# Row sums of 16,384 rows on one core: 16-row blocks, loads alternating between two rings, a last block in shrinking pieces

## The chip, the cores and the metric

One core of one Trainium2 chip runs the kernel. The metric is the device time of one execution in microseconds (us); the span of a run in its profile is 1.6 to 2.1 us shorter. All runs quoted are fast (the granted clock is 1.0 in all), and most runs of one kernel lie within 0.3% of one another. Ratios and their intervals compare fast runs of the same rounds on the same chip, and differ by less than 0.001 from the ratio of the medians quoted beside them.

Names: VectorE is DVE in the profile and ScalarE is ACT. SyncE (SP) only issues loads and stores here. "SPq" and "ACTq" are the instruction sequencers of SyncE and ScalarE, which issue transfers; each feeds a ring (a queue of transfers) of its own, and both rings are served by the same 16 DMA engines. A load "lands" when it is reported complete, some 0.4 us after its last packet ends.

## The reference, cut to what matters

```python
batch, seq, dim = 32, 512, 1024           # x: float32, 67.1 MB
def reference(x, multiplier):             # multiplier = 0.5
    return (np.sum(x, axis=-1) * multiplier).astype(np.float32)
```

Each of the 128 partitions owns 128 consecutive rows of 4 KiB, so any group of n rows is one contiguous run of n x 4 KiB per partition.

## The kernel before

It loads 15 blocks of 8 rows per partition (4 MiB each) through three buffers, all from SyncE's ring, and then a taper of 2, 2, 1, 1, 1, 1 rows. VectorE reduces seven rows of each block in one instruction, and ScalarE sums the eighth with an activation that accumulates.

```python
taper = [(2, "s"), (2, "s"), (1, "s"), (1, "v"), (1, "v"), (1, "v")]
big_rows = 8
big_pool = ctx.enter_context(tc.tile_pool(name="big", bufs=3))
...
for _ in range(n_big):                                    # 15 times
    x_tile = big_pool.tile([P, big_rows, D], fp32, name="x_tile_b")
    nc.sync.dma_start(out=x_tile, in_=x_rows[:, c0 : c0 + big_rows, :])
    nc.vector.reduce_sum(out=staging[:, c0 : c0 + 7], in_=x_tile[:, 0:7, :], ...)
    nc.vector.tensor_single_scalar(...)                   # times 0.5
    scalar_row_sum(x_tile, 7, c0 + 7)                     # ScalarE: one row
    c0 += big_rows
for sz, eng in taper:
    ...                                                   # load sz rows, sum on ScalarE or VectorE
nc.sync.dma_start(out=out_view, in_=out_sbuf)
```

The compiled program is not laid out in source order: the framework orders each engine's instructions itself. Each engine works its list off in order: in e11 below VectorE leaves a block that landed at 134.78 us untouched until 142.07, since an earlier block in its list had not landed.

## Time and profile before

The median of the first three runs was 164.76 us.

| | before |
|---|---|
| span of the profiled run | 163.1 us |
| a 32 KiB packet (one partition's 8 rows), median of the packet records | 1,213 ns |
| packet time per DMA engine, sum of the records over 16 | 157.6 us |
| big blocks land every | 9.7 to 9.85 us |
| reduction of 7 rows on VectorE | 7.62 us |
| last landing of data, then to the end | 159.82 us, 3.3 us |

From the page of the kernel before: the span, the busy time of the engines, then two rows with one value for each of 40 equal slices of the span (the busy tenths of the DMA engines, and the GB/s they moved), the share of the ring, and the costliest group.

```profile
span 163.1 us, 170 instructions
...
DVE 118.8 (73%) x36; ACT 23.9 (15%) x41; POOL 0.2 (0%) x4
...
DMA  6999999999999999999999999999999999998990
GB/s 193 442 402 458 434 386 466 426 394 466 418 402 466 426 394 466 434 410 466 410 450 434 402 466 426 410 458 426 426 450 410 434 450 402 466 426 368 413 382 19
...
q1 hardware_dynamic: 3168, 67.18, 96.6%
...
L78 DVE TENSOR_REDUCE staging<-x_tile_b 128x7 f32<-128x7168 f32 x15 | 114.3, 7620 | 40.3 <-DMA x_tile_b<-in_x_dram 40.3
```

The DMA row is the one to read: 9 tenths or more from the second slice to nearly the last. A packet of 32 KiB in 1,213 ns on each of 16 engines is 432 GB/s. The Trainium skill ("DMA: Bandwidth & Descriptors", "Where 436 GB/s comes from") puts the ceiling of the ports into SBUF at 435 GB/s, and the trace agrees; the lower figure that the same section gives for loads from HBM, about 358 GB/s, does not limit this run on one core. VectorE's last column says what it waits for: 40.3 us in all, always the load.

The chain of waits of the kernel before (start, length, what), that is, the chain of work that ended last:

```profile
by line: DMA x_tile_b<-in_x_dram 58.8%; DVE staging L78 18.7%; DMA x_tile_s<-in_x_dram 17.6%; SPq L97 1.3%; SPq L76 0.7%; DVE x_tile_s L62 0.4%; issue 0.4%; DVEq L137 0.0%
...
33.02 7.63 DVE staging L78
40.66 0.02 SPq L76
...
40.71 21.65 DMA x_tile_b<-in_x_dram
...
62.38 7.63 DVE staging L78
...
131.09 28.73 DMA x_tile_s<-in_x_dram
...
159.85 0.69 DVE x_tile_s L62
```

The chain alternates between 21 us of transfer and 7.63 us of reduction, which looks as if VectorE were on the path for 19% of the span. It is not: the reduction frees a buffer and so starts a load, but two other loads are queued in that time, and the engines stay full. The chain shows who released whom; whether a resource ran dry is seen only in the row of slices.

Its last line is the sum of the last row on VectorE, 0.69 us, right after the last landing.

### The profile page before, as it was taken

The page shows a single profiled execution, that of the slowest core. Times are in us where ns is not written, and L with a number is a line of the kernel's source. Part 1 is how long each engine was busy: PE and PEld are TensorE (multiplying, and loading weights), DVE is VectorE, ACT ScalarE, POOL GpSimd, SP SyncE. Part 2 cuts the span into 40 slices and gives each one's busy share as a digit, 9 for nine tenths or more (in the row PEclk, how much of TensorE's full clock was granted, in tenths as well). Part 3 has the DMA queues.
Part 4 walks back from the last instruction along what each step waited for, and adds up shares of the span by engine and source line. Part 5 has one row for each costly group of instructions (what it writes and reads, how often), then busy time and mean ns, then how long its engine had stood idle before and what let it go on. Part 6 is the DMA issues. An engine that isn't in the chain of part 4 may idle for free.

```text
span 163.1 us, 170 instructions
## 1 busy us (share of the span) xinstructions
DVE 118.8 (73%) x36; ACT 23.9 (15%) x41; POOL 0.2 (0%) x4
## 2 busy tenths in 40 slices
DVE  0007949699595987959599595977959598695982
ACT  3002020020200202020020201102020020202670
POOL 0000000000000000000000000000000000000000
DMA  6999999999999999999999999999999999998990
GB/s 193 442 402 458 434 386 466 426 394 466 418 402 466 426 394 466 434 410 466 410 450 434 402 466 426 410 458 426 426 450 410 434 450 402 466 426 368 413 382 19
DMA packets 3168, 67.18 MB, mean 412 GB/s; under 512 B 352, under 2 KB 480, under 8 KB 992
## 3 DMA queue, kind: packets, MB, share of 16 engines
q1 hardware_dynamic: 3168, 67.18, 96.6%
HBM read 67.11 MB, written 0.07 MB: 412 GB/s over the span
## 4 chain that ended last, share of the span: by engine, by line
DMA 76%; DVE 19%; SPq 2%; issue 0%; DVEq 0%
DMA x_tile_b<-in_x_dram 59%; DVE staging L78 19%; DMA x_tile_s<-in_x_dram 18%; SPq L97 1%; SPq L76 1%; DVE x_tile_s L62 0%; DVEq L137 0%
## 5 line engine op out<-in xcount | busy, mean ns | idle before, releaser
L78 DVE TENSOR_REDUCE staging<-x_tile_b 128x7 f32<-128x7168 f32 x15 | 114.3, 7620 | 40.3 <-DMA x_tile_b<-in_x_dram 40.3
L53 ACT ACTIVATE x_tile_b<-x_tile_b 128x1024 f32<-128x1024 f32 x15 | 15.8, 1057 | 131.8 <-DMA x_tile_b<-in_x_dram 131.8
L53 ACT ACTIVATE x_tile_s<-x_tile_s 128x1024 f32<-128x1024 f32 x5 | 5.2, 1046 | 1.6 <-DMA x_tile_s<-in_x_dram 1.6
L83 DVE TENSOR_SCALAR out_sbuf<-staging 128x7 f32<-128x7 f32 x15 | 2.6, 170 | 0.5
L53 ACT ACTIVATION_READ_ACCUMULATOR x_tile_b<-x_tile_b 128x1 f32 x15 | 2.8, 187 | 0.0
L62 DVE CUSTOM_DVE_ANT_0 x_tile_s<-x_tile_s 128x512 f32<-128x512 f32 x3 | 2.1, 689 | 0.9 <-DMA x_tile_s<-in_x_dram 0.9
L53 ACT ACT_TABLE_LOAD x1 | 1.3, 1283 | 0.7 <-PEq L123 0.7
L53 ACT ACTIVATION_READ_ACCUMULATOR x_tile_s<-x_tile_s 128x1 f32 x5 | 0.9, 186 | 0.0
L62 DVE DVE_READ_ACCUMULATOR2_ANT out_sbuf<- 128x1 f32 x3 | 0.2, 82 | 0.0
L123 POOL MEMSET const-uint8-127<- 128x1 uint8 x1 | 0.1, 103 | 0.0
L123 POOL MEMSET const-bfloat16-1.0<- 128x1 bf16 x1 | 0.1, 102 | 0.0
L123 POOL MEMSET const-float32-0.0<- 128x1 f32 x1 | 0.1, 99 | 0.2 <-issue 0.2
L123 POOL MEMSET const-float32-1.0<- 128x1 f32 x1 | 0.1, 99 | 0.0
## 6 DMA issues: line engine op xcount, KB each, us to landing
x_tile_b<-in_x_dram SPq DMA_DIRECT2D x15, 4096.0 KB, 21.4
x_tile_s<-in_x_dram SPq DMA_DIRECT2D x2, 1024.0 KB, 24.5
x_tile_s<-in_x_dram SPq DMA_DIRECT2D x4, 512.0 KB, 27.6
out_dram<-out_sbuf SPq DMA_DIRECT2D x1, 64.0 KB, 1.5
```

Of the source, the lines that this page charges most:

```text
L53: nc.scalar.activation(out=x_tile[:, r, :], in_=x_tile[:, r, :], func=mybir.ActivationFunctionType.Copy, scale=mul, accum_out=out_sbuf[:, ...
L62: nc.vector.tensor_tensor_reduce(out=x_tile[:, r, 0:H], in0=x_tile[:, r, 0:H], in1=x_tile[:, r, H:D], scale=mul, scalar=0.0, op0=mybir.Alu ...
L76: nc.sync.dma_start(out=x_tile, in_=x_rows[:, c0 : c0 + big_rows, :])
L78: nc.vector.reduce_sum(out=staging[:, c0 : c0 + vec_rows_per_big], in_=x_tile[:, 0:vec_rows_per_big, :], axis=mybir.AxisListType.X,)
L83: nc.vector.tensor_single_scalar(out=out_sbuf[:, c0 : c0 + vec_rows_per_big], in_=staging[:, c0 : c0 + vec_rows_per_big], scalar=mul, op=m ...
L97: nc.sync.dma_start(out=x_tile, in_=x_rows[:, c0 : c0 + sz, :])
L123: nc = _bacc.Bacc("TRN2", target_bir_lowering=False, num_devices=1)
```

## The change

The intent: fewer and longer transfers (64 KiB per partition instead of 32), two rings to issue them, the compute split evenly between VectorE and ScalarE, and a last block that arrives in ever smaller pieces, so that little work is left after the last byte. The diff, cut to its core:

```diff
-    big_rows = 8
-    big_pool = ctx.enter_context(tc.tile_pool(name="big", bufs=3))
+    B = 16                                   # 8 blocks
+    x_pool = ctx.enter_context(tc.tile_pool(name="x", bufs=3))
 ...
-    for _ in range(n_big):
-        nc.sync.dma_start(out=x_tile, in_=x_rows[:, c0 : c0 + big_rows, :])
-        (VectorE: rows 0..6, ScalarE: row 7)
+    for b in range(n_blocks - 1):            # blocks 0..6
+        c0 = b * B
+        t = x_pool.tile([P, B, D], fp32, name="xb")
+        (nc.scalar if b % 2 else nc.sync).dma_start(
+            out=t, in_=x_rows[:, c0 : c0 + B, :]
+        )
+        (VectorE: rows 0..7, ScalarE: rows 8..15)
 ...
-    (taper: 2, 2, 1, 1, 1, 1 rows)
+    pieces = [(0, 8), (8, 12), (12, 14), (14, 15)]    # rows of block 7
+    for lo, hi in pieces:
+        nc.sync.dma_start(out=t[:, lo:hi, :], in_=x_rows[:, c0 + lo : c0 + hi, :])
+    for lo, hi in ((0, 768), (768, 1024)):            # its last row, in two
+        nc.sync.dma_start(out=t[:, 15, lo:hi], in_=x_rows[:, c0 + 15, lo:hi])
+    (rows 4..7, 10, 11, 13 on ScalarE, the rest on VectorE)
+    dve_span(t, B - 1, 0, cut, part)
+    dve_span(t, B - 1, cut, D, res[:, rows - 1 : rows], start=part)
```

More of the change, by code (lines that the diff above doesn't have):

```diff
@@ L5 @@
 import concourse.tile as tile
-from concourse import bass_utils, mybir
+from concourse import mybir
 from concourse._compat import with_exitstack
@@ L20 @@
     fp32 = mybir.dt.float32
+    ADD = mybir.AluOpType.add
     x_flat = x.flatten_outer_dims()
     N, D = x_flat.shape
-    H = D // 2
-    out_flat = out.rearrange("b s -> (b s)")
-    assert N % P == 0
-    rows_per_part = N // P
-    taper = [(2, "s"), (2, "s"), (1, "s"), (1, "v"), (1, "v"), (1, "v")]
-    taper_rows = sum(sz for sz, _ in taper)
-    big_rows = 8
-    assert (rows_per_part - taper_rows) % big_rows == 0
-    n_big = (rows_per_part - taper_rows) // big_rows
-    scalar_rows_per_big = 1
@@ L37 @@
-    vec_rows_per_big = big_rows - scalar_rows_per_big
-    x_rows = x_flat.rearrange("(p c) d -> p c d", p=P)
-    out_view = out_flat.rearrange("(p c) -> p c", p=P)
-    big_pool = ctx.enter_context(tc.tile_pool(name="big", bufs=3))
-    small_pool = ctx.enter_context(tc.tile_pool(name="small", bufs=4))
-    res_pool = ctx.enter_context(tc.tile_pool(name="res", bufs=1))
-    small_bufs = {2: 2, 1: 4}
-    staging = res_pool.tile([P, rows_per_part], fp32)
-    out_sbuf = res_pool.tile([P, rows_per_part], fp32)
@@ L50 @@
-    mul = float(multiplier)
-    def scalar_row_sum(x_tile, r, col):
+    rows = N // P
+    x_rows = x_flat.rearrange("(p c) d -> p c d", p=P)
+    out_view = out.rearrange("b s -> (b s)").rearrange("(p c) -> p c", p=P)
+    mul = float(multiplier)
+    B = 16
+    n_blocks = rows // B
+    assert N == P * rows and rows == n_blocks * B
+    x_pool = ctx.enter_context(tc.tile_pool(name="x", bufs=3))
+    res_pool = ctx.enter_context(tc.tile_pool(name="res", bufs=1))
+    sums = res_pool.tile([P, rows], fp32, name="sums")
@@ L53, in scalar_row_sum, with act_row, dve_span @@
+    res = res_pool.tile([P, rows], fp32, name="res")
+    part = res_pool.tile([P, 1], fp32, name="part")
+    def act_row(t, r, col):
         nc.scalar.activation(
-            out=x_tile[:, r, :],
-            in_=x_tile[:, r, :],
+            out=t[:, r, :],
+            in_=t[:, r, :],
             func=mybir.ActivationFunctionType.Copy,
             scale=mul,
-            accum_out=out_sbuf[:, col : col + 1],
+            accum_out=res[:, col : col + 1],
         )
-    def vector_row_sum(x_tile, r, col):
+    def dve_span(t, r, lo, hi, dst, start=0.0):
+        mid = (lo + hi) // 2
@@ L62, in vector_row_sum @@
         nc.vector.tensor_tensor_reduce(
-            out=x_tile[:, r, 0:H],
-            in0=x_tile[:, r, 0:H],
-            in1=x_tile[:, r, H:D],
+            out=t[:, r, lo:mid],
+            in0=t[:, r, lo:mid],
+            in1=t[:, r, mid:hi],
             scale=mul,
-            scalar=0.0,
-            op0=mybir.AluOpType.add,
-            op1=mybir.AluOpType.add,
-            accum_out=out_sbuf[:, col : col + 1],
-        )
-    c0 = 0
-    for _ in range(n_big):
-        x_tile = big_pool.tile([P, big_rows, D], fp32, name="x_tile_b")
-        nc.sync.dma_start(out=x_tile, in_=x_rows[:, c0 : c0 + big_rows, :])
+            scalar=start,
@@ L78 @@
+            op0=ADD,
+            op1=ADD,
+            accum_out=dst,
+        )
+    for b in range(n_blocks - 1):
[4 more added lines that the diff above has]
+        )
+        h = B // 2
         nc.vector.reduce_sum(
-            out=staging[:, c0 : c0 + vec_rows_per_big],
-            in_=x_tile[:, 0:vec_rows_per_big, :],
-            axis=mybir.AxisListType.X,
+            out=sums[:, c0 : c0 + h], in_=t[:, 0:h, :], axis=mybir.AxisListType.X
@@ L82 @@
         )
         nc.vector.tensor_single_scalar(
-            out=out_sbuf[:, c0 : c0 + vec_rows_per_big],
-            in_=staging[:, c0 : c0 + vec_rows_per_big],
+            out=res[:, c0 : c0 + h],
+            in_=sums[:, c0 : c0 + h],
             scalar=mul,
@@ L88 @@
         )
-        for r in range(vec_rows_per_big, big_rows):
-            scalar_row_sum(x_tile, r, c0 + r)
-        c0 += big_rows
-    for sz, eng in taper:
-        x_tile = small_pool.tile(
-            [P, sz, D], fp32, name=f"x_tile_s{sz}", tag=f"s{sz}", bufs=small_bufs[sz]
-        )
-        nc.sync.dma_start(out=x_tile, in_=x_rows[:, c0 : c0 + sz, :])
-        for r in range(sz):
-            if eng == "s":
-                scalar_row_sum(x_tile, r, c0 + r)
-            else:
-                vector_row_sum(x_tile, r, c0 + r)
-        c0 += sz
-    assert c0 == rows_per_part
-    nc.sync.dma_start(out=out_view, in_=out_sbuf)
+        for r in range(h, B):
+            act_row(t, r, c0 + r)
+    c0 = (n_blocks - 1) * B
+    t = x_pool.tile([P, B, D], fp32, name="xb")
+    cut = 768
+    pieces = [(0, 8), (8, 12), (12, 14), (14, 15)]
+    for lo, hi in pieces:
+        nc.sync.dma_start(out=t[:, lo:hi, :], in_=x_rows[:, c0 + lo : c0 + hi, :])
+    for lo, hi in ((0, cut), (cut, D)):
+        nc.sync.dma_start(
+            out=t[:, B - 1, lo:hi], in_=x_rows[:, c0 + B - 1, lo:hi]
+        )
+    on_act = {4, 5, 6, 7, 10, 11, 13}
+    for r in range(B - 1):
+        if r in on_act:
+            act_row(t, r, c0 + r)
+        else:
+            dve_span(t, r, 0, D, res[:, c0 + r : c0 + r + 1])
+    dve_span(t, B - 1, 0, cut, part)
+    dve_span(t, B - 1, cut, D, res[:, rows - 1 : rows], start=part)
+    nc.sync.dma_start(out=out_view, in_=res)
 _INS = ['x', 'multiplier']
```

## The prediction

> **What bounds it now.** The DMA engines. In the page's 40 slices DMA is at 9 tenths nearly throughout; the 16 engines are 96.6% taken, while VectorE is busy 73% and ScalarE 15%. In the groups view the seven-row reduction takes 7.62 us, but a 4 MiB block lands only every 9.7 to 9.85 us, so VectorE waits about 2 us per block, always for the load. The chain of waits names VectorE for 19%, but only because a buffer's release starts a load; two other loads are queued then, and the engines never run dry. In the packet records a 32 KiB row takes 1,213 ns (median), times 16 engines 432 GB/s. The Trainium skill ("DMA: Bandwidth & Descriptors", "Where 436 GB/s comes from") puts the ceiling at 435 GB/s; this trace agrees. So about 157.6 us of the 163.1 us span is packet time per engine. Outside it: first packet at 1.97 us, its longer first packet (about 2.0 us), and after the last landing (159.82) one 0.69 us custom row sum, 0.35 us to issue the store, 1.5 us for it to land and the end.
>
> **What the change does.**
> 1. Bytes: the same 67.1 MB. No gain.
> 2. Longer packets. From 4 KiB packets (161 ns) and 32 KiB packets (1,213 ns) I work out a fixed 10 ns or so per packet. Halving the packet count of the big blocks, about 56 fewer packets per engine, is worth about 0.6 us (estimate).
> 3. Two rings. Both feed the same 16 engines (same page, "Issuing engines are not separate DMA queues"), so no bandwidth. Blocks 0 and 1 will share the engines and land almost together at about 39 to 42 us, instead of one at 22; compute starts far later. That costs nothing as long as some load is always queued: three 8 MiB buffers, 19.4 us of transfer per block, and about 9 us of compute.
> 4. Compute per block: 8 rows on VectorE, about 8.7 us + 0.17; 8 on ScalarE at a pitch of 1.06 us, about 8.5 us. Both are well below 19.4 us. Off the critical path.
> 5. Tail: the last piece is 256 columns, so the last custom instruction halves 256 to 128: about 0.3 us instead of 0.69 (estimate from 0.69 us at 512). Worth 0.4 us, on the path. The landings in the last block stay at the engines' rate.
> 6. ScalarE is in order and now issues loads. If its stream puts a load behind activations that wait for an earlier block, rings run dry: about 9 us each time, and with the first one already late the kernel could come to 175 to 195 us. I expect that the loads are placed ahead of those activations, as they are ready first.
>
> **Prediction.** 164.76 - 0.6 - 0.4, with a little lost to mixing: 163.9 us, 163.0 to 166.5 in 8 of 10. Faster by over 2%: 0.03 (the packet time alone forbids it); within 2%: 0.81; slower: 0.16.
>
> **What would show it.** Right: DMA share still about 97%, about 430 GB/s in every middle slice; the first reduction only near 40 us, landings in pairs; VectorE idle mostly for DMA; 64 KiB packets of about 2.41 us; last custom op near 0.3 us. Wrong on 2: packets still 32 KiB, or over 2.43 us. Wrong on 3 and 6: slices of DMA well below 9 in the middle of the span, with ScalarE's load issues standing after activations.
>
> **What would make it wrong.** The order of ScalarE's instructions (6); a rate that two interleaved streams lower or raise; late buffer release when blocks land in pairs; a last block that waits for its buffer.

## The result, and the profile after

The changed kernel takes 175.65 us (175.50 to 175.76), against 165.07 us for the kernel before in the same rounds: a ratio of 1.0637, with a 95% interval from 1.0604 to 1.0669. It is 6% slower.

From the page of the changed kernel: the span, busy times, the slices of VectorE, ScalarE and the DMA engines, their GB/s, and the shares of the two rings (q1 is SyncE's, q10 ScalarE's).

```profile
span 174.0 us, 233 instructions
...
DVE 67.0 (39%) x34; ACT 67.2 (39%) x127; POOL 0.2 (0%) x4
...
DVE  0000000002999700990000999900000000999992
ACT  2000000002999500980000999800000000999994
...
DMA  6999899988999799998999508999889997999900
GB/s 241 482 482 392 362 452 482 482 377 347 482 482 422 331 452 482 482 409 362 437 482 482 241 0 316 407 482 482 377 347 482 482 482 309 414 403 422 379 2 15
...
q1 hardware_dynamic: 1584, 42.01, 57.1%
q10 hardware_dynamic: 432, 25.17, 33.5%
```

The DMA engines have a hole in the middle (slices 23 to 25: 241, 0 and 316 GB/s) and fall silent two slices before the end, while VectorE and ScalarE are at 9 tenths through the hole and up to the last slice. The bytes cost what they did: the packet records add up to 157.5 us per engine, against 157.6. So all of the loss is time in which the DMA engines had nothing to do. Windows on the changed kernel (stretch and its length, then busy time of each engine with its instructions, clock, DMA share and GB/s) confirm both stretches:

```profile
core 0: us, DVE busy (x) ACT busy (x) POOL busy (x), PEclk, DMA share, GB/s
100.50:105.50 5.00, 5.00 (x2) 5.00 (x11) 0.00 (x0) 1.00 0.00 0
165.50:173.00 7.50, 5.11 (x18) 5.97 (x12) 0.00 (x0) 1.00 0.03 9
```

The loss of 10.9 us in the span (174.0 - 163.1) has two parts, read from the landing records. The last data lands at 165.86 us instead of 159.82, which is 6.0 us later. From there to the end it takes 8.1 us instead of 3.3, which is 4.9 us more.

The chain of waits of the changed kernel:

```profile
by line: DMA xb<-in_x_dram 72.1%; ACT xb L48 25.0%; issue 1.0%; ACTq L138 0.1%
...
52.90 42.94 DMA xb<-in_x_dram
...
95.86 10.54 ACT xb L48 x21
...
106.44 40.99 DMA xb<-in_x_dram
...
147.45 2.25 ACT xb L48 x5
...
166.27 5.20 ACT xb L48 x10
```

Where the chain before ran through the loads and single reductions, this one runs through long strings of activations on ScalarE (25% of the span), and each string ends in the issue of a load (52.90, 106.44), or in the end of the kernel. The timeline (start, length, engine, line, operation, operands, and in brackets the idle time before and who ended it) shows what these two loads are:

```profile
52.90 0.33 ACTq L72 DMA_DIRECT2D xb<-in_x_dram  x1
...
78.14 0.17 DVE L79 TENSOR_SCALAR res<-sums 128x8 f32<-128x8 f32 x1
95.86 1.06 ACT L48 ACTIVATE xb<-xb 128x1024 f32<-128x1024 f32 x1 [18.02 <-DMA xb<-in_x_dram]
95.86 17.28 DVE L76 TENSOR_REDUCE sums<-xb 128x8 f32<-128x8192 f32 x2 [17.55 <-DMA xb<-in_x_dram]
...
106.44 0.33 ACTq L72 DMA_DIRECT2D xb<-in_x_dram  x1
...
147.45 17.28 DVE L76 TENSOR_REDUCE sums<-xb 128x8 f32<-128x8192 f32 x2 [34.10 <-DMA xb<-in_x_dram]
```

The load at 52.90 is that of block 3, the one at 106.44 that of block 5. Block 5 goes into the buffer of block 2, whose last reader finished at about 78 us (VectorE's reduction of it ends where its scaling begins, at 78.14). The load could go out then. It goes out 28 us later. The listing of the compiled program gives ScalarE's list in order:

```
DMACopy    xb <- in_x_dram 128x16384          (block 1)
LoadActFuncSet
Activation xb,res <- xb 128x1024 x16          (blocks 0, 1)
DMACopy    xb <- in_x_dram 128x16384          (block 3)
Activation xb,res <- xb 128x1024 x24          (blocks 2, 3, 4)
DMACopy    xb <- in_x_dram 128x16384          (block 5)
Activation xb,res <- xb 128x1024 x23          (blocks 5, 6, 7)
```

Block 5's load stands behind the activations of blocks 3 and 4, which can't run before those blocks have landed, at 95.84 and 100.92 us. (It is issued at 106.44 us, five activations ahead of its place in the list: the last activation of block 4 ends at 112.5 us. So the sequencer ran that far ahead of the engine.) SyncE's ring doesn't help, for it is waiting too: block 6 needs the buffer of block 3, which VectorE frees at 104.6 us.

SyncE's side of the timeline, around the hole:

```profile
104.62 0.33 SPq L72 DMA_DIRECT2D xb<-in_x_dram  x1
113.20 1.83 SPq L93 DMA_DIRECT2D xb<-in_x_dram  x4
```

So from 100.48 to 105.58 us no packet is in flight on any engine. When loads go out again, blocks 5 and 6 go out within 2 us of each other on two rings and share the engines: they land at 147.43 and 143.75 us, and 17 us of work start at 147.45 with block 7 still to come.

### The profile page after: what moved, and what is told of

Its sections match the earlier page's. It is cut to its first block, busy times and chain, and to the rows that moved or that the text cites. A ratio compares the mean times of both kernels' runs of the same rounds, so it can differ in the third digit from the quotient of the medians.

```text
span 174.0 us, 233 instructions
## 1 busy us (share of the span) xinstructions
DVE 67.0 (39%) x34; ACT 67.2 (39%) x127; POOL 0.2 (0%) x4
## 4 chain that ended last, share of the span: by engine, by line
DMA 72%; ACT 25%; issue 1%; ACTq 0%
DMA xb<-in_x_dram 72%; ACT xb L48 25%; ACTq L138 0%
## 5 line engine op out<-in xcount | busy, mean ns | idle before, releaser
L48 ACT ACTIVATE xb<-xb 128x1024 f32<-128x1024 f32 x63 | 65.5, 1041 | 103.1 <-DMA xb<-in_x_dram 103.1
L76 DVE TENSOR_REDUCE sums<-xb 128x8 f32<-128x8192 f32 x7 | 60.5, 8682 | 103.6 <-DMA xb<-in_x_dram 103.6
L48 ACT ACTIVATION_READ_ACCUMULATOR xb<-xb 128x1 f32 x63 | 11.8, 187 | 0.0
L58 DVE CUSTOM_DVE_ANT_0 xb<-xb 128x512 f32<-128x512 f32 (+1 forms) x9 | 5.5, 674 | 0.0
L79 DVE TENSOR_SCALAR res<-sums 128x8 f32<-128x8 f32 x7 | 1.1, 167 | 0.0
L58 DVE DVE_READ_ACCUMULATOR2_ANT res<- 128x1 f32 x9 | 0.8, 85 | 0.0
```

The source lines that it names most:

```text
L48: nc.scalar.activation(out=t[:, r, :], in_=t[:, r, :], func=mybir.ActivationFunctionType.Copy, scale=mul, accum_out=res[:, col : col + 1],)
L58: nc.vector.tensor_tensor_reduce(out=t[:, r, lo:mid], in0=t[:, r, lo:mid], in1=t[:, r, mid:hi], scale=mul, scalar=start, op0=ADD, op1=ADD, ...
L76: nc.vector.reduce_sum(out=sums[:, c0 : c0 + h], in_=t[:, 0:h, :], axis=mybir.AxisListType.X)
L79: nc.vector.tensor_single_scalar(out=res[:, c0 : c0 + h], in_=sums[:, c0 : c0 + h], scalar=mul, op=mybir.AluOpType.mult,)
```

## The experiments

Twelve kernels ran; all gave correct results. The theory (A) was that the cause is the place of loads in ScalarE's list. The rivals were that blocks of 16 rows in three buffers are too coarse (B), that packets of 64 KiB are slower (C), or that two rings cost in themselves, by making blocks land in pairs (D).

| run | what differs from the changed kernel | us, median | ratio to before, 95% interval |
|---|---|---|---|
| e1_one_ring | every load on SyncE | 164.07 | 0.9964 (0.9950 to 0.9977) |
| e2_block5_sync | block 5 alone moved to SyncE | 163.97 | 0.9963 (0.9947 to 0.9978) |
| e3_block1_act | only block 1 left on ScalarE | 163.97 | 0.9958 (0.9945 to 0.9972) |
| e4_act_order | same rings, loads earlier in ScalarE's list | 163.95 | 0.9958 (0.9944 to 0.9971) |
| e5_block5_late | only block 5 left on ScalarE | 164.01 | 0.9962 (0.9948 to 0.9976) |
| e6_late_in_order | blocks 6 and 7 on ScalarE too | 177.65 | 1.0791 (1.0774 to 1.0807) |
| e7_row_whole | e1, last row in one piece | 164.20 | 0.9972 (0.9959 to 0.9984) |
| e8_cut512 | e1, last row cut at 512 | 163.95 | 0.9955 (0.9943 to 0.9968) |
| e9_32k_packets | e1, each load as two of 8 rows | 164.47 | 0.9980 (0.9966 to 0.9994) |
| e10_split_first | e8, block 0 as two half loads | 183.68 | 1.1147 (1.1132 to 1.1162) |
| e11_late_forced | e5, the load forced behind block 4 | 170.11 | 1.0334 (1.0317 to 1.0352) |
| e12_six_before_five | sums of block 6 before those of 5 | 172.23 | 1.0470 (1.0454 to 1.0485) |

Median times of the kernel before beside them: 164.68 (e1 to e4), 164.71 (e5 to e8), 164.79 (e9, e10) and 164.56 us (e11, e12).

### All loads on one ring

```diff
-        (nc.scalar if b % 2 else nc.sync).dma_start(
+        nc.sync.dma_start(
```

> The changed kernel with every load on the SyncE ring; blocks of 16 rows, 64 KiB rows and the shrinking last block stay. Theory A (the 11 us come from ScalarE's ring alone: the load of block 5 stands behind the activations of blocks 3 and 4, the engines run dry at 100 to 105 us, and blocks 5 and 6 land together at 147 us): no dry stretch, landings 19.4 us apart from about 23 us on, last landing near 159.5 us, 163.5 to 165.0 us in all. Rival B (16-row blocks with three buffers are too coarse whatever the ring): about 175 us, with a dry stretch or a tail after the last landing of over 6 us. Rival C (64 KiB packets are slower): the landings 20 us or more apart, 167 us or more.

It took 164.07 us. The blocks land at 23.07, 42.45, 61.80, 81.32, 100.65, 119.99 and 139.34 us, that is, every 19.3 to 19.5 us, and the last piece at 159.00. The DMA row of the page of the one-ring version:

```profile
DMA  6969979979979979989998998998998998998990
```

The row swings between 7 and 9 tenths, and it is down to 6 once near the start. This is not idle time: the row counts a packet wholly in the slice in which it starts, and a packet now takes 2.4 us, more than half a slice of 4.1 us, so the slices catch packets unevenly. From the first load on, the packet records have no moment without a packet in flight until the last data packet ends at 158.56 us, and there is no 0 or 5 as in the changed kernel. B falls: the blocks and buffers are the same. C falls too: 64 KiB packets take 2,418 ns (median), just under twice 1,213. What was lost had to do with ScalarE's ring.

### One load moved, and one load left

```diff
-        (nc.scalar if b % 2 else nc.sync).dma_start(
+        (nc.scalar if b in (1, 3) else nc.sync).dma_start(      # e2
+        (nc.scalar if b == 1 else nc.sync).dma_start(           # e3
```

> The changed kernel with block 5 alone moved from ScalarE's ring to SyncE's; blocks 1 and 3 still come by ScalarE's ring. Theory A: the load of block 5 goes out at about 78 us, when VectorE has finished block 2, instead of 106 us; no dry stretch; 163.5 to 166 us. Rival D (two rings in themselves cost, through landings in pairs and a backlog of compute at the end): still 170 us or more.

> The changed kernel with block 1 alone on ScalarE's ring. Theory A: blocks 0 and 1 still share the engines and land together at about 42 us, which costs nothing, as a third load is queued: 163.5 to 165.5 us. Rival D: the late start of compute (42 instead of 23 us) costs: 168 us or more.

Both took 163.97 us. In e2 the DMA engines have no gap, though blocks 0 and 1 still land together (42.50 and 42.67 us) and blocks 3 and 4 nearly so (96.05 and 101.06). In e3 blocks 0 and 1 land at 42.29 and 42.46 us. So it was the load of block 5 alone; that compute starts at 42 instead of 23 us costs nothing, and D falls as far as pairs in the middle go. The shared landing is what the Trainium skill ("DMA: Bandwidth & Descriptors", "Queues, rings and completion order") lets one expect: each engine takes whole packets from its rings in turn. The trace agrees: with one ring the first block landed at 23.07 us, with two in use at 42.29.

### The same rings, another order

```diff
+    for b in range(3):
+        load(b)                                  # the same ring for each block as in the change
+    for b in range(n_blocks - 1):
+        if b >= 1 and (b + 2) % 2 and b + 2 < n_blocks - 1:
+            with tc.issue_after(loads[b + 2].ins):
+                compute(b)                       # activations of b behind the load of b + 2
+        else:
+            compute(b)
+        if b + 3 < n_blocks - 1:
+            load(b + 3)
```

> The changed kernel with the same rings for the same blocks, but ScalarE's instructions in another order: the load of block 3 straight after the activations of block 0, that of block 5 straight after those of block 2 (before: after those of blocks 1 and 4). Theory A: the load of block 5 goes out near 80 us, no dry stretch, blocks 5 and 6 no longer land together, 163.5 to 165.5 us. Rival D (two rings cost in themselves): 168 us or more.

It took 163.95 us. ScalarE's list is now: load 1, 8 activations, load 3, 16 activations, load 5, 39 activations. From its timeline:

```profile
51.18 0.34 ACTq L74 DMA_DIRECT2D xb<-in_x_dram  x1
...
77.83 0.17 DVE L84 TENSOR_SCALAR res<-sums 128x8 f32<-128x8 f32 x1
77.88 0.33 ACTq L74 DMA_DIRECT2D xb<-in_x_dram  x1
...
132.09 8.69 DVE L81 TENSOR_REDUCE sums<-xb 128x8 f32<-128x8192 f32 x1 [15.50 <-DMA xb<-in_x_dram]
```

The load of block 5 goes out at 77.88 us, 0.05 us after VectorE's scaling of block 2 starts, instead of 106.44. Nothing else about rings, blocks or buffers was changed. (Block 3's load moved too, from 52.90 to 51.18 us; e2 shows that moving block 5's alone is enough.) This is the most direct proof of A: the two rings are harmless when a load doesn't stand behind activations that wait for something later.

### Which half of the loss is which

Is the late load costly only through the hole, or also through the backlog at the end? The first try to separate them failed in its design:

```diff
-        (nc.scalar if b % 2 else nc.sync).dma_start(
+        (nc.scalar if b == 5 else nc.sync).dma_start(
```

> One ring for all loads but that of block 5, which stays in ScalarE's stream, where it stands behind the activations of block 4. Block 6 is by then in flight on SyncE's ring (issued at about 90 us), so the engines should not run dry, but block 5, issued near 104 us, then shares the engines with blocks 6 and 7 and lands late, near 144 us, while the compute of block 6 waits behind it. If the late landing alone costs: last landing still near 159.5 us, but some 8 to 9 us of work after it instead of 3.2; 171 to 173.5 us in all. If only a dry stretch costs: 164 to 165 us.

It took 164.01 us, because the load was not late: with the other two loads gone from ScalarE's list, the framework put block 5's behind 24 activations (blocks 0 to 2) and not behind 40, and it went out at 70.55 us. I had misread the listing. As it stands, the run is one more case in which a load on ScalarE's ring in good time costs nothing. The next run forces the place with an ordering edge:

```diff
+        if b == 5:
+            with tc.issue_after(acts[4].ins):    # last activation of block 4
+                nc.scalar.dma_start(out=t, in_=x_rows[:, c0 : c0 + B, :])
+        else:
+            nc.sync.dma_start(out=t, in_=x_rows[:, c0 : c0 + B, :])
```

> What the run with block 5 alone on ScalarE's ring was meant to be: there the load stood behind block 2's activations and was not late. Here an ordering edge puts it behind block 4's last activation, as in the changed kernel; all other loads are on SyncE's ring. Block 6 is in flight by then (issued near 90 us), so no dry stretch. If a late landing alone costs: block 5 lands near 144 us, the last landing stays near 159 to 160 us, 8 to 9 us of work follow it instead of 3.2, 171 to 173.5 us in all. If only a dry stretch costs: 164 to 165 us.

It took 170.11 us, a little less than I expected. There is no gap in the middle, and the last data lands at 159.28 us, as in the fast versions; but 9.3 us follow (span 168.6), against 3.2 in e1. From its timeline, the late load and the start of VectorE's work on block 5 (the store follows at 166.11 us):

```profile
103.29 0.37 ACTq L76 DMA_DIRECT2D xb<-in_x_dram  x1
...
142.07 17.28 DVE L80 TENSOR_REDUCE sums<-xb 128x8 f32<-128x8192 f32 x2 [32.23 <-DMA xb<-in_x_dram]
```

Block 5 lands at 142.05 us. The other load in flight had landed at 134.78, but VectorE's line shows no work until 142.07: the engines work the blocks off in program order. Blocks 5, 6 and 7 are all worked off after 142 us. So a backlog costs by itself, without any dry stretch.

For the other half, blocks 6 and 7 were put on ScalarE's ring as well, behind block 5:

```diff
-        (nc.scalar if b % 2 else nc.sync).dma_start(
+        (nc.scalar if b in (1, 3, 5, 6) else nc.sync).dma_start(
 ...
-        nc.sync.dma_start(out=t[:, lo:hi, :], ...)      # block 7's pieces
+        nc.scalar.dma_start(out=t[:, lo:hi, :], ...)
```

> The changed kernel, with blocks 6 and 7 put on ScalarE's ring too, behind block 5, whose load stays where the changed kernel has it, behind the activations of block 4. The dry stretch stays (about 101 to 108 us, a little longer than the 100.5 to 105.6 of the changed kernel, as nothing else restarts the engines), but the last three blocks come in order. If the dry stretch costs by itself: last landing near 166 to 167 us, 3 to 3.5 us after it, 170.5 to 172.5 us in all. If only the backlog costs: 164 to 166 us.

It took 177.65 us, more than expected. From its chain of waits:

```profile
106.65 41.16 DMA xb<-in_x_dram
...
150.11 0.33 ACTq L93
...
152.41 19.86 DMA xb<-in_x_dram
```

The engines are dry twice: from 99.99 to 107.19 us, as expected, and from 147.47 to 151.09, which I had not foreseen. Block 7's pieces stand behind the activations of blocks 5 and 6 in ScalarE's list and go out from 150.11 us on, though VectorE was done with block 4, whose buffer they use, at 113 us. The last data lands at 172.58 us, and 3.2 us follow (span 175.8). So dry stretches cost by themselves as well: 7.2 + 3.6 us of silence in a kernel whose last landing is 13.6 us later than e1's. And the same fault has struck a second load.

The last of this group leaves the hole and changes only the order of the sums:

```diff
+    with tc.issue_after(last.ins):   # block 5's load behind block 4's activations, as in the change
+        t5 = load(5)
+    t6 = load(6)
+    last = compute(6, t6)
+    with tc.issue_after(last.ins):
+        compute(5, t5)
```

> The changed kernel with the same loads in the same places, but the sums of block 6 ahead of those of block 5, since block 6 landed 3.7 us before it (143.75 and 147.43 us). The dry stretch stays. If the backlog at the end, worked off in order, is on the path: the work after the last landing shrinks from 8.6 us to about 5 us and the time to about 172 us. If not: 175.6 us.

It took 172.23 us, 3.4 us less than the changed kernel by the medians, 3.6 us by the spans (170.4 and 174.0) and some 2.8 us by the two ratios to the kernel before. From its timeline:

```profile
106.39 0.35 ACTq L72 DMA_DIRECT2D xb<-in_x_dram  x1
...
143.74 17.28 DVE L80 TENSOR_REDUCE sums<-xb 128x8 f32<-128x8192 f32 x2 [30.45 <-DMA xb<-in_x_dram]
```

The load is just as late (106.39), the hole is there (100.32 to 105.54 us), and the last data lands at 165.80; but VectorE starts at 143.74 instead of 147.45, and 4.6 us follow the last landing instead of 8.1. (The 8.6 us of the expectation seem to count from the end of the last packet, not from the landing.) The backlog is on the path.

### The small terms: last row and packet length

```diff
-    for lo, hi in ((0, cut), (cut, D)):          # e7: the last row in one piece
+    for lo, hi in ((0, D),):
-    dve_span(t, B - 1, 0, cut, part)
-    dve_span(t, B - 1, cut, D, res[:, rows - 1 : rows], start=part)
+    dve_span(t, B - 1, 0, D, res[:, rows - 1 : rows])

-    cut = 768                                    # e8
+    cut = 512
```

> All loads on one ring, and the last row in one piece instead of 768 and 256 columns. If the cut saves nothing, since the op on 256 columns waits for the op on 768 columns and not for its load: within 0.15 us of the version with the cut (164.07 us), the last custom op taking 0.69 us and starting at its landing. If the cut saves the 0.35 us of my prediction: 164.4 us.

> All loads on one ring, and the last row cut into 512 and 512 columns. The second piece now lands about 0.6 us after the first, while the first op takes about 0.42 us and its accumulator 0.1, so the second op should start at its landing and take about 0.42 us: the work after the last landing 0.2 to 0.3 us shorter than with 768 and 256, 163.7 to 164.0 us. Close to the noise; the time from last landing to end in the profile decides.

They took 164.20 and 163.95 us, against 164.07 for the cut at 768; the intervals of the ratios overlap, so only the traces decide. The two last operations of e1 (cut at 768; 384 and 128 are the half widths that the operation adds up):

```profile
158.71 0.56 DVE L58 CUSTOM_DVE_ANT_0 xb<-xb 128x384 f32<-128x384 f32 x1 [0.25 <-DMA xb<-in_x_dram]
...
159.31 0.35 DVE L58 CUSTOM_DVE_ANT_0 xb<-xb,part 128x128 f32<-128x128 f32 x1
```

The pieces land at 158.68 and 159.00 us, 0.32 us apart. The operation on the first takes 0.56 us, so the one on the second can't start at its landing; it starts 0.31 us after it and ends 0.66 us after it. With the whole row (e7) the single operation of 0.69 us starts 0.02 us after the landing at 159.05 and ends 0.71 us after it. The cut at 768 is thus worth 0.05 us. With the cut at 512 (e8):

```profile
158.38 0.43 DVE L58 CUSTOM_DVE_ANT_0 xb<-xb 128x256 f32<-128x256 f32 x1
...
159.10 0.48 DVE L58 CUSTOM_DVE_ANT_0 xb<-xb,part 128x256 f32<-128x256 f32 x1 [0.29 <-DMA xb<-in_x_dram]
```

The pieces land at 158.35 and 158.97 us. The first operation is done in time, but the second, which takes the first one's sum as its start value, takes 0.48 us and begins 0.13 us after its landing: it ends 0.61 us after it. That is worth 0.05 us more, where I expected 0.2 to 0.3.

```diff
-        nc.sync.dma_start(out=t, in_=x_rows[:, c0 : c0 + B, :])
+        for k in range(0, B, 8):                 # e9: 32 KiB packets again
+            nc.sync.dma_start(
+                out=t[:, k : k + 8, :], in_=x_rows[:, c0 + k : c0 + k + 8, :]
+            )
```

> All loads on one ring, each 16-row load issued as two of 8 rows into the same buffer: packets of 32 KiB as before the change, all else as in the one-ring version (164.07 us). If the longer packets are what saves (my 0.6 us): 164.5 to 164.9 us, and the packets' sum per engine about 0.5 us up from 156.0. If not: 163.9 to 164.3 us.

It took 164.47 us, and its interval (0.9966 to 0.9994) overlaps that of e1, so the time alone doesn't decide. The packet sum is 157.1 us per engine, against 156.0 in e1 and 156.4 in e7 and e8, and the last data lands at 159.29 us, against 159.00, 159.05 and 158.97. The longer packets seem to be worth about 0.3 us at the last landing, and as much by the ratios (0.9980 against 0.9964). But each landing is that of a single profile, and that of e2, also with 64 KiB packets but on two rings, came at 159.43 us, so the size is not firm.

### A version that was to be better, and was not

```diff
+        if b == 0:                               # e10, on top of e8
+            for e, p in ((nc.sync, 0), (nc.scalar, P // 2)):
+                e.dma_start(out=t[p : p + P // 2], in_=x_rows[p : p + P // 2, 0:B, :])
```

> The one-ring version with the last row cut at 512, and with block 0 loaded as two halves of 64 partitions, one from each ring at the same moment. In the traces the 16 engines start their first packets one after another over 0.95 us, and this stagger stays to the last landing; two half loads should halve it. If so: first packets within about 0.5 us of one another, the last landing 0.3 to 0.5 us earlier, 163.3 to 163.8 us. If the halves collide instead: 164 us or more.

It took 183.68 us. The GB/s row of its page:

```profile
GB/s 231 231 231 231 231 187 173 173 173 447 461 447 432 360 375 461 461 461 461 461 418 404 360 434 461 461 461 461 403 418 389 403 461 461 375 432 404 427 399 54
```

For the first nine slices the engines move about half of what they move later. Both halves of block 0 landed only at 43.09 and 43.26 us, where the whole block landed at 22.97 in e8, and their 64 KiB packets took some 4.9 us each instead of 2.4. The Trainium skill ("SBUF — State Buffer", "Door 1: The DMA port swizzle") says that partitions 0 to 63 reach only 8 of the 16 ports through which data enters SBUF, and partitions 64 to 127 the other 8. Halves on two rings at the same time could have used all 16. But the packet records show the rings served in turn: 16 packets of SyncE's half start between 2.05 and 3.27 us, 16 of ScalarE's between 6.45 and 7.94, 16 of SyncE's from 11.36 on, and so to the end of the block. Most of the time, then, nearly all engines write into the same half, which fits the doubled packet time; that the ports are the cause was not tested apart. The stagger of the first packets didn't shrink either: they spread over 1.22 us.

The version to keep is any of e1 to e5 or e8: some 0.4% faster than the kernel before, with intervals that exclude 1. I would take e8, with one ring, as nothing in it depends on where the framework places a load in a compute engine's list.

## Why the prediction was wrong

- **What bounds the kernel, and point 1 (bytes): right.** The packet records sum to 157.6 us per engine before and 157.5 after. No kernel here got below 163.75 us in any run. (A slip without weight: the first large packet starts at 1.73 us in the records, not at 1.97.)
- **Point 6 is the step that failed.** "I expect that the loads are placed ahead of those activations, as they are ready first." That held for block 1's load, which stands ahead of all activations, and for block 3's in effect (52.90 us, against 51.18 in e4), but not for block 5's, which went out at 106.44 us instead of 77.88 (e4). The prediction named the mechanism and a size for the hole ("about 9 us each time", with 175 to 195 us if it happens), gave a slower kernel 16 in 100, and left it out of the range. That 175.65 us lies within 175 to 195 is in part luck: the hole measured 5.1 us and not 9, and the rest of the loss is the backlog, which this step didn't have. From the source alone it could not be told for sure; but in the source the load of block 5 stands after the activations of blocks 0 to 4, and that it would be moved ahead of them was an assumption that no view of the old profile supported. The old kernel issues no load from an engine that also computes, so its trace could not show it.
- **Point 3 (two rings): the mechanism was right**, that blocks 0 and 1 land together at 39 to 42 us (42.29 and 42.46 measured) at no cost (e2, e3, e4). Its condition, "as long as some load is always queued", did not hold from 100.48 to 105.58 us.
- **Point 4 (compute off the critical path): wrong in the changed kernel**, and that is the second half of the loss. I had allowed for two blocks landing together in the middle, but not at the end, where no transfer is left to hide 17 us of work: 8.1 us after the last landing instead of 3.3. With the load in time (e4) the point holds.
- **Point 2 (longer packets, 0.6 us): the right sign**, but about half the size, some 0.3 us at the last landing (e9 against e1, e7 and e8).
- **Point 5 (tail, 0.4 us): wrong.** The last operation did shrink, from 0.69 to 0.35 us, but it waits for the operation before it and not for its load; what the cut saves is 0.05 us (e1 against e7). The term left out was the 0.56 us of the first piece.
- The number itself, 163.9 us, is what e1 to e5 and e8 measure (163.95 to 164.07). It was the time of a kernel whose loads go out when their buffers are free. That it fits so well is in part luck: terms 2 and 5 as measured come to some 0.35 us, not 1.0, while these kernels gain 0.6 to 0.8 us on the medians of the kernel before in their rounds; no run explains the rest.

What stays open: why the framework moved block 1's load ahead of earlier blocks' activations, but left block 5's behind. That is decided when the program is built, and no run here shows it; e4, e5 and e6 only show that the place moves with what else is in the list.

## What to carry to other kernels

A load issued from an engine that also computes is only as early as its place in that engine's list: before trusting it, read the list, and ask of each load whether something ahead of it waits for data that comes later than the buffer it needs. When a kernel is bound by its transfers, look for slices in which the DMA engines are idle before looking at anything else, and then count what work is left after the last landing. Before cutting the last piece smaller, compare the operations with the gap between the landings: here the cut at 768 (0.56 us against a gap of 0.32) saved 0.05 us over the whole row, and the cut at 512 (0.43 against 0.62) only 0.10.

## What the Trainium skill lacked or had wrong

- "DMA: Bandwidth & Descriptors", "Issuing engines are not separate DMA queues": it says that issuing from several engines only saves issue time. It lacks the risk: a load on a compute engine's ring can stand behind that engine's work. Here one load was 28.6 us late (106.44 against 77.88 us) and the kernel lost 6.4%; issue itself took 0.33 us.
- The same page, "Queues, rings and completion order": the switching between rings at packets is there, but not what it does to landings: two blocks of 8 MiB issued together landed at 42.29 and 42.46 us on two rings, and at 23.07 and 42.45 on one.
- The same page, "Rules for kernel authors": it calls two transfers to disjoint partition halves not worth the bother, since they serialize. The run bears this out; what this row lacks is the cost, which has to be worked out from the ports of the page cited above: a block of 8 MiB in two halves landed at 43.26 us, against 22.97 for the whole block in one load.
- No page gives packet times by row length for these rings: 1,213 ns for 32 KiB and 2,418 ns for 64 KiB (medians), so the longer row gains only 0.3% per byte.
- No page that I know of says that the 16 engines start one after another: in the kernel before their first packets began over 0.95 us (1.73 to 2.68 us).
